# A different maker for the low parts of two groups of weights in an fp32 encoder

## The chip, the cores and the metric

The kernel runs on one core of a Trainium2 chip. A core has a matrix engine, TensorE (PE in the profile, its weight loads PEld), and VectorE (DVE), ScalarE (ACT), GpSimd (POOL) and SyncE (SP). Each works through its own list of instructions in order and waits on semaphores for the others. Matmul operands lie in SBUF and results in PSUM; DMA transfers are issued by SP and by POOL, each through its own queue. The metric is the device time of one execution in microseconds (us).

## The reference

Two layers of a transformer-like encoder on 512 tokens of width 1024, in fp32:

```python
for l in range(DEPTH):                                    # DEPTH = 2
    x = x + 0.5 * swiglu(rms_norm(x, ffn1_norm[l]), w_gate, w_up, w_down)
    h = rms_norm(x, mix_norm[l])
    p = h @ w_in[l]
    attn = mla_group(p[..., :o_kv], p[..., o_kv:o_pe], p[..., o_pe:o_cv], ...)
    conv = conv_group(p[..., o_cv:], ...)                 # GLU, causal convolution of 31 taps, LayerNorm, SiLU
    x = x + jnp.concatenate([attn, conv], axis=-1) @ w_out[l]
    x = x + 0.5 * swiglu(rms_norm(x, ffn2_norm[l]), w_gate, w_up, w_down)
    x = rms_norm(x, post_norm[l])
...
def swiglu(x, w_gate, w_up, w_down):
    return (jax.nn.silu(x @ w_gate) * (x @ w_up)) @ w_down  # hidden width 2816 = 22 x 128
```

## The kernel before

**Three matmuls for one.** Each fp32 operand is kept as two parts in a shorter format, `hi` (the value rounded by an ACT copy) and `lo` (what the rounding left). `mm3` does a product as hi·hi (L209), hi·lo of the activations (L210) and lo of the weights·hi (L211). So each weight tile, loaded from memory as plain fp32 into a buffer `raw` or `fr`, is split before use.

**Two ways to make a weight's low part.** The usual one: DVE subtracts `hi` from the loaded tile, in `load_w` at L164 and in `split_into` at L301. The other one: ACT writes the negative of the loaded tile's rounded value, and a DMA issued by POOL adds the same weights from memory on top of it. In `load_w` this is the kind `"sum"` (L160 and L161), in the FFN it is `subtracted` (L432 and L433), called by `summed`. In the first form of it the low part lies in the tile `weights`, a ring of four slots for `hi` and four for `lo`, whose writers are kept in their order by `in_turn`. In the second it lies in a buffer of the pool `ls`, of which there are two:

```python
lo = fpool.tile([P, WC], FR, tag="ls", name=nm("ls"), bufs=2)
```

**The FFN.** The 22 blocks of the hidden width are taken as 11 pairs, in chunks of 2, 3, 3, 2 and 1 pairs. `pair` makes one pair's activations by a scheme of seven products in place of eight, with quarters of the weights combined by DVE; two of its seven products (`b21`, `t4`) use `ls`. `down` multiplies a chunk's activations by the down weights in two halves `g`, also in seven products each: `b11` (quarter 0 of the weights), `b21` (quarter 1), `t2`, `t3`, `t1` (combinations), `t4` (quarter 3) and `b22`. Within `down`, `times` is one product; with a number `q` it takes `summed`, without one `split_into`. Before, `b21` and `t4` took `summed`, and the ACT copy and the DMA for `t4` were issued early, by `subtracted` ahead of `t3`. Quarters 0 and 1 are loaded by SP and later overwritten by the combinations.

**The two-pair stage.** The chunk of pairs 8 and 9 is the only one for which `np_`, the number of pairs in `down`, is 2; the others have `NP` = 3. Its weights are `wdr` (256 KB a quarter, 512 columns). It occurs in the first FFN of both layers and in the second FFN of the last one; the second FFN of the first layer joins the chunk with the next one and has no such stage. In the order of PE the pair after it (pair 10, `held`) stands ahead of the stage's `down`, and that pair's `t4` is the last reader of an `ls` buffer ahead of it. A tile scheduler sets the order of all instructions from the order in the code, its own estimates and the marks `issue_after`.

**The mixer's start.** `mix_body` begins with `groups` on the first two blocks `wcv` of the convolution's projection (512 KB each), and calls `norm` right after. While PE multiplies these, ACT squares the new `x` (L242) for the norm, POOL sums the squares (L246), and DVE makes the last low parts of the input (L223, in `split_scaled`) behind the residual sums of the FFN's end (L634).

Of the kernel before, what the change touches and what calls it, by code (L numbers as in the profile page):

```python
# [33 lines left out]
WC = 1024  # L34
# [6 lines left out]
NP = 3  # L41
# [42 lines left out]
def encoder_kernel(ctx: ExitStack, tc: tile.TileContext, xT, consts, vecs, rgain, wgu1, wd1, wdq1, wdr1,  # L84
# [11 lines left out]
    def nm(s):  # L96
        uid[0] += 1
        return f"{s}{uid[0]}"
# [7 lines left out]
    def bank():  # L106
        return psum.tile([P, S], FP, tag="ps", name=nm("ps"))
# [45 lines left out]
    def load_w(src, w, kind=""):  # L153
        raw = wpool.tile([P, WC], FP, tag="raw", name=nm("raw"), bufs=3)
        nc.sync.dma_start(out=raw[:, :w], in_=src)
        hi = part(0)
        order["cast"] = in_turn("h", lambda: A.copy(hi[:, :w], raw[:, :w]))  # L157
        lo = low()
        if kind == "sum":
            A.activation(lo[:, :w], raw[:, :w], AF.Copy, scale=-1.0)  # L160
            G.dma_start(out=lo[:, :w], in_=src, accum_op=ALU.add)  # L161
            return hi, lo
        e = G if kind in POOLW.split() else V
        in_turn(e, lambda: e.tensor_tensor(lo[:, :w], raw[:, :w], hi[:, :w].bitcast(FP), ALU.subtract))  # L164
        return hi, lo
# [4 lines left out]
    def part(j, moved=False):  # L170

        if was[j] and not moved:
            used[j] += 1
        was[j] = moved
        i = (j * WN + used[j] % WN) * WC + (WOFF[j] if moved else 0)
        used[j] += 1
        return weights[:, i:i + WC]
# [3 lines left out]
    def in_turn(key, make):  # L181

        with tc.issue_after(turns[key]) if key in turns else nullcontext():
            turns[key] = make().ins
        return turns[key]

    def low(moved=False):
        return part(1, moved)
# [19 lines left out]
    def mm3(o, lh, ll, rh, rl, first, last, free=False):  # L208
        T.matmul(o, lh, rh, start=first, stop=False, skip_group_check=free)  # L209
        T.matmul(o, lh, rl, start=False, stop=False, skip_group_check=free)  # L210
        order["mm"] = T.matmul(o, ll, rh, start=False, stop=last, skip_group_check=free).ins  # L211
        return order["mm"]
# [68 lines left out]
    def group(o, w, rhs, ks, n, ts=slice(0, S)):  # L281

        for k in ks:
            c = slice(k * P, (k + 1) * P)
            order["product"] = mm3(o, w[0][:, c], w[1][:, c], rhs[k][0][:, ts], rhs[k][1][:, ts], k == 0, k == n - 1)

    def groups(srcs, rhs, ws=None):

        ws = ws or [load_w(src, WC) for src in srcs]
        os = [bank() for _ in srcs]  # L290
        for ks in (range(KD - 1), range(KD - 1, KD)):
            for o, w in zip(os, ws):
                group(o, w, rhs, ks, KD)
        return os

    def split_into(q, src, w=WC):

        hi = part(0, True)
        in_turn("h", lambda: A.copy(hi[:, :w], src[:, :w]))  # L299
        lo = low(True)  # L300
        order["lo"] = in_turn(V, lambda: V.tensor_tensor(lo[:, :w], src[:, :w], hi[:, :w].bitcast(FP), ALU.subtract))  # L301
        return hi, lo
# [5 lines left out]
    def ffn_body(fpool, l, gx, norm, wgu, wd, wdq, wdr, gain, done, w0, halved, chunks):  # L308
# [20 lines left out]
        def quarters(w, n, first=False):  # L329

            a = quarter(), quarter() if first else late(), quarter(), quarter()
            for q in range(4):
                nc.sync.dma_start(out=a[q][:, :n], in_=w[q])
            return *a, late()
# [26 lines left out]
        def after(name):  # L361
            return tc.issue_after(order[name]) if name in order else nullcontext()
# [66 lines left out]
        def subtracted(w, src, n=WC):  # L429

            lo = fpool.tile([P, WC], FR, tag="ls", name=nm("ls"), bufs=2)
            A.activation(lo[:, :n], src[:, :n], AF.Copy, scale=-1.0)  # L432
            G.dma_start(out=lo[:, :n], in_=w, accum_op=ALU.add)  # L433
            return lo

        def summed(w, src, n=WC, lo=None):

            lo = subtracted(w, src, n) if lo is None else lo
            hi = part(0, True)
            in_turn("h", lambda: A.copy(hi[:, :n], src[:, :n]))  # L440
            return hi, lo
# [54 lines left out]
        def down(act, quarters_of):  # L496

            np_ = len(act)
            n = 2 * np_ * P
            for g in range(2):  # L500
                a11, a12, a21, a22, s3 = quarters(quarters_of(g), n)
                px, py, pz = bank(), bank(), bank()

                def times(o, src, name, start, q=None, lo=None):
                    hi, lo = split_into(name, src, n) if q is None else summed(quarters_of(g)[q], src, n, lo)
                    with tc.issue_after(order["pe"]):
                        for k in range(np_):
                            for i in range(2):
                                c = slice((i * np_ + k) * P, (i * np_ + k + 1) * P)
                                last = mm3(o[:, i * HS:(i + 1) * HS], hi[:, c], lo[:, c], *act[k][name],  # L510
                                           start and k == 0 and i == 0, k == np_ - 1, True)
                    order["pe"] = last

                def add(row, h, o, sign):
                    v = x[:, 4 * g + 2 * (1 - row):4 * g + 2 * (1 - row) + 2, h * HS:(h + 1) * HS]
                    return V.scalar_tensor_tensor(v, o.rearrange("p (m t) -> p m t", m=2), 0.5 * sign, v, ALU.mult,  # L516
                                                  ALU.add).ins
                times(px, a11, "b11", True)
                with after("u0"):
                    add(0, 0, px, 1)  # L520
                times(py, a12, "b21", True, 1)
                with after("u"):
                    add(0, 0, py, 1)
                with after("first") if g else nullcontext():
                    V.tensor_tensor(s3[:, :n], a11[:, :n], a21[:, :n], ALU.add)
                with after("first"):
                    V.tensor_tensor(a21[:, :n], a21[:, :n], a22[:, :n], ALU.add)
                    V.tensor_tensor(a11[:, :n], a11[:, :n], a21[:, :n], ALU.add)
                times(px, a11, "t2", False)
                order["second"] = add(1, 0, px, -1)  # L530
                with after("second" if g == 0 else "first"):
                    V.tensor_tensor(a12[:, :n], a12[:, :n], a11[:, :n], ALU.add)  # L532
                lo = subtracted(quarters_of(g)[3], a22, n)
                with after("u"):
                    times(pz, s3, "t3", True)
                add(1, 1, pz, 1)
                with after("v"), after("vh"):
                    times(px, a21, "t1", False)
                    order["first"] = add(1, 1, px, -1)
                    times(pz, a22, "t4", False, 3, lo)  # L540
                    add(1, 0, pz, 1)
                with after("v"), after("vh"):
                    times(px, a12, "b22", False)
                add(0, 1, px, 1)
# [13 lines left out]
        for p0, p1 in chunks:  # L558
# [46 lines left out]
            if p0 and not last:  # L605
                c = (p0 - CHUNKS[0][1]) // NP
                if p1 == chunks[-1][0] and p1 == CHUNKS[-1][0]:
                    held = pair(p1, False)
                down(act, (lambda g: wdq[l, g, c]) if c < NC else (lambda g: wdr[l, g]))
                continue  # L610
# [47 lines left out]
    def mix(l, gx, norm, done):  # L658
        with tc.tile_pool(name="k", bufs=4) as kpool:
            mix_body(kpool, l, gx, norm, done)  # L660

    def mix_body(kpool, l, gx, norm, done):
# [191 lines left out]
                                            ALU.mult).ins  # L854


        first = groups([wcv[l, 0], wcv[l, 1]], gx)
        rm = norm()
        for step in SEQ.split():
            if step == "R":  # L860
# [272 lines left out]
    gx = []  # L1133
# [21 lines left out]
    gx = [gx[KS.index(m)] for m in range(KD)]  # L1155
# [27 lines left out]
    for l in range(L):  # L1183
        nx, st1, done = follow(l, "gm")
        ffn(l, gx, norm, wgu1, wd1, wdq1, wdr1, vv(l, "g1"), done, w0 if l == 0 else None)
        gx = nx
        nx, st2, done = follow(l, "g2")
        mix(l, gx, Norm(st1), done)
        gx = nx
# [3 lines left out]
        if l + 1 < L:  # L1193
# [10 lines left out]
            gx = nx  # L1204
# [126 lines left out]
```

## Time and profile before

| | us |
|---|---|
| median of three runs (lowest, highest) | 1750.08 (1748.02, 1750.13) |
| the profiled execution | 1748.6 |
| its span, first to last instruction | 1746.8 |
| PE busy | 1729.1 |
| DVE busy | 1468.6 |
| ACT busy | 1097.4 |
| POOL busy | 394.2 |

The mean granted clock of TensorE was 0.998 of full speed. In the page's rows a time is the start of an instruction in us from the span's start, followed by its duration, engine, line of the program, operation, output <- inputs by the program's names, and shapes. A bracket at the end gives the idle time of that engine before the instruction and what ended it. Several like instructions that follow one another may share a row (x2). A row of a DMA issue gives the size and the median time from issue to landing.

### The profile page before, as it was taken

What the parts mean: (1) busy time and instruction counts of PE and PEld (TensorE: products, weight loads), DVE (VectorE), ACT (ScalarE), POOL (GpSimd) and SP (SyncE); (2) the same over time, 40 slices, a digit from 0 to 9 for tenths busy, and PEclk for the clock granted to TensorE, in tenths of its full rate; (3) what the DMA queues carried; (4) which work ended last, traced back from release to release, by engine and by line L of the source; (5) the groups of instructions that cost most, each with busy time, mean ns of one, the idle gap of its engine ahead of it and who ended that gap; (6) DMA issues with size and microseconds to landing.
All of it is one profiled execution on the core that took longest, in us unless ns stands there. A gap on an engine that the chain in (4) does not pass through costs nothing.

```text
span 1746.8 us, 31487 instructions
## 1 busy us (share of the span) xinstructions
PE 1729.1 (99%) x12486; PEld 1580.1 (90%) x12486; DVE 1468.6 (84%) x2099; ACT 1097.4 (63%) x1711; POOL 394.2 (23%) x327
## 2 busy tenths in 40 slices
PE   9999999999999999999999999999999999999998
PEld 8899999888678899999889999997976788999997
DVE  7888888888965989897679989888989568888887
ACT  5576756567953476756645757665778435767564
POOL 1001000348823001000310010013676410010002
PEclk9999999999999999999999999999999999999999
DMA  5567575424303467665426575754251125675753
GB/s 184 148 151 187 140 198 112 135 87 118 80 25 102 115 161 176 158 173 138 124 71 162 133 203 132 196 121 130 83 147 36 58 81 147 153 188 139 194 117 98
DMA packets 76852, 231.57 MB, mean 133 GB/s; under 512 B 8736, under 2 KB 12960, under 8 KB 76704
## 3 DMA queue, kind: packets, MB, share of 16 engines
q1 hardware_dynamic: 58704, 171.87, 30.8%
q0 software_dynamic: 17856, 57.68, 19.4%
q8 instruction: 98, 1.61, 0.4%
q14 instruction: 50, 0.41, 0.1%
q10 hardware_dynamic: 144, 0.00, 0.0%
HBM read 225.33 MB, written 2.10 MB: 130 GB/s over the span
## 4 chain that ended last, share of the span: by engine, by line
PE 69%; DVE 7%; ACT 2%; issue 2%; DMA 1%; DVEq 0%; ACTq 0%
PE ps L211 22%; PE ps L209 22%; PE ps L210 22%; DVE cv L999 1%; DVE mx L907 1%; PE ps L948 1%; PE ps L926 1%; DVE x L516 0%; DVE weights L164 0%; ACT weights L299 0%; PE ps L705 0%; DVE x L634 0%; DVE r L929 0%; DMA fr<-in_wgu 0%; ACT pr L1003 0%
## 5 line engine op out<-in xcount | busy, mean ns | idle before, releaser
L210 PE MATMUL ps<-r,weights 128*128 128x256 f32 (+1 forms) x2620 | 810.6, 309 | 2.6 <-DVE r L223 2.6
L209 PE MATMUL ps<-r,weights 128*128 128x256 f32 (+1 forms) x2620 | 807.5, 311 | 0.2
L211 PE MATMUL ps<-r,weights 128*128 128x256 f32 (+1 forms) x2380 | 741.2, 313 | 6.0 <-DVE weights L301 3.7
L210 PEld LDWEIGHTS ps<-r,weights 128*128 128x128 f32 x2620 | 492.1, 188 | 35.5 <-DVE r L223 4.4
L209 PEld LDWEIGHTS ps<-r,weights 128*128 128x128 f32 x2620 | 492.2, 188 | 33.4 <-issue 2.0
L211 PEld LDWEIGHTS ps<-r,weights 128*128 128x128 f32 x2380 | 446.8, 188 | 38.6 <-DVE weights L301 5.0
L209 PE MATMUL ps<-xj,weights 128*128 128x256 f32 x864 | 238.5, 276 | 0.0
L210 PE MATMUL ps<-xj,weights 128*128 128x256 f32 x864 | 238.5, 276 | 0.0
L299 ACT CAST weights<-fr 128x1024 fp32r<-128x1024 f32 (+2 forms) x178 | 168.5, 946 | 96.7 <-DVE fr L453 43.0
L157 ACT CAST weights<-raw 128x1024 fp32r<-128x1024 f32 (+4 forms) x124 | 112.1, 916 | 176.1 <-PE ps L210 112.3
L301 DVE TENSOR_TENSOR weights<-fr,weights 128x1024 fp32r<-128x1024 f32 (+2 forms) x178 | 195.4, 1098 | 31.5 <-ACT weights L299 31.5
L433 POOL DMA_DIRECT2D ls<-in_wgu x72 | 62.5, 868 | 703.7 <-ACT ls L432 633.3
L164 DVE TENSOR_TENSOR weights<-raw,weights 128x1024 fp32r<-128x1024 f32 (+4 forms) x108 | 120.8, 1126 | 65.1 <-ACT weights L157 64.3
L210 PEld LDWEIGHTS ps<-xj,weights 128*128 128x128 f32 x864 | 162.2, 188 | 0.0
L209 PEld LDWEIGHTS ps<-xj,weights 128*128 128x128 f32 x864 | 162.2, 188 | 0.0
L211 PE MATMUL ps<-xj,ls 128*128 128x256 f32 x576 | 159.0, 276 | 0.0
L301 DVE TENSOR_TENSOR weights<-raw,weights 128x1024 fp32r<-128x1024 f32 (+2 forms) x112 | 122.1, 1091 | 14.1 <-ACT weights L299 13.9
L299 ACT CAST weights<-raw 128x1024 fp32r<-128x1024 f32 (+2 forms) x112 | 105.2, 939 | 42.8 <-DVE raw L532 23.5
L1005 POOL TENSOR_TENSOR y<-y,pr 128x495 f32<-128x495 f32 (+29 forms) x90 | 119.3, 1329 | 45.8 <-ACT pr L1003 40.5
L432 ACT ACTIVATE ls<-fr 128x1024 fp32r<-128x1024 f32 (+2 forms) x62 | 59.9, 967 | 98.7 <-PE ps L211 63.0
L516 DVE SCALAR_TENSOR_TENSOR x<-ps,x 128x512 f32<-128x512 f32 x154 | 105.8, 687 | 8.7 <-PE ps L211 7.8
L211 PEld LDWEIGHTS ps<-xj,ls 128*128 128x128 f32 x576 | 108.1, 188 | 0.0
(260 smaller groups left out, 3021.0 us busy)
## 6 DMA issues: line engine op xcount, KB each, us to landing
fr<-in_wgu SPq DMA_DIRECT2D x112, 512.0 KB, 4.7
ls<-in_wgu POOLq DMA_DIRECT2D x72, 512.0 KB, 7.1
raw<-in_wgu SPq DMA_DIRECT2D x62, 512.0 KB, 5.3
fr<-in_wdq SPq DMA_DIRECT2D x48, 384.0 KB, 4.5
ls<-in_wdq POOLq DMA_DIRECT2D x32, 384.0 KB, 6.3
raw<-in_wd SPq DMA_DIRECT2D x32, 256.0 KB, 2.8
raw<-in_wcv SPq DMA_DIRECT2D x16, 512.0 KB, 3.8
raw<-in_wout SPq DMA_DIRECT2D x16, 512.0 KB, 3.3
```

The costliest lines, as they stand in the source:

```text
L157: order["cast"] = in_turn("h", lambda: A.copy(hi[:, :w], raw[:, :w]))
L164: in_turn(e, lambda: e.tensor_tensor(lo[:, :w], raw[:, :w], hi[:, :w].bitcast(FP), ALU.subtract))
L209: T.matmul(o, lh, rh, start=first, stop=False, skip_group_check=free)
L210: T.matmul(o, lh, rl, start=False, stop=False, skip_group_check=free)
L211: order["mm"] = T.matmul(o, ll, rh, start=False, stop=last, skip_group_check=free).ins
L299: in_turn("h", lambda: A.copy(hi[:, :w], src[:, :w]))
L301: order["lo"] = in_turn(V, lambda: V.tensor_tensor(lo[:, :w], src[:, :w], hi[:, :w].bitcast(FP), ALU.subtract))
L432: A.activation(lo[:, :n], src[:, :n], AF.Copy, scale=-1.0)
L433: G.dma_start(out=lo[:, :n], in_=w, accum_op=ALU.add)
L516: return V.scalar_tensor_tensor(v, o.rearrange("p (m t) -> p m t", m=2), 0.5 * sign, v, ALU.mult, ALU.add).ins
L907: V.tensor_reduce(mx[:, i:i + 1], o, axis=AX.X, op=ALU.max, negate=True)
L1005: order["conv"] = G.tensor_tensor(ys[c][:, s:], ys[c][:, s:], pr[:, s:], ALU.add).ins
```

## The change

The first product of each half of the two-pair stage, `b11`, gets its weights' low part by `summed` in place of `split_into`; stages with three pairs stay as they are. And the first two blocks of the convolution's projection are loaded with the kind `"sum"` in each layer.

```diff
@@ down
-                times(px, a11, "b11", True)
+                times(px, a11, "b11", True, 0 if np_ < NP else None)
@@ mix_body
-        first = groups([wcv[l, 0], wcv[l, 1]], gx)
+        first = groups([wcv[l, 0], wcv[l, 1]], gx, [load_w(wcv[l, i], WC, "sum") for i in range(2)])
```

Over the program DVE has 10 instructions less, ACT 10 more and POOL 8 more rows of DMA issues and sums (the two DMAs of a layer's mixer share a row). The order of SP is the same.

On ACT, in the two-pair stage of the first layer's first FFN, one piece of the difference (`fr_3522` is quarter 0 of the first half, `raw_3523` quarter 1, `fr_3525` quarter 3):

```order
 L457 ACTIVATE t_3367<-t_3332 128x256
 L216 CAST r_3290<-t_3281 128x512
-L299 CAST weights<-fr_3522 128x512
+L440 CAST weights<-fr_3522 128x512
 L426 COPY t_3424<-ps_3305 128x512
 L440 CAST weights<-raw_3523 128x512
 L426 COPY e_3396<-ps_3303 128x512
-L432 ACTIVATE ls_3585<-fr_3525 128x512
+L432 ACTIVATE ls_3551<-raw_3523 128x512
 L299 CAST weights<-fr_3522 128x512
 L471 ACTIVATE t_3483<-e_3396 128x512
```

The L432 that stands here made the operand of `t4` before, and makes that of `b21` now; the one ahead of this piece made `b21`'s before and makes `b11`'s now.

On ACT at the start of the first layer's mixer (`raw_` of L157 is a `wcv` block). Before:

```order
L196 CAST weights_106<-raw395_3776 128x1024
L157 CAST weights_106<-raw447_3931 128x1024
L157 CAST weights_106<-raw448_3935 128x1024
L222 ACTIVATE r397_3788<-x_74,vec_76 128x512
L239 ACTIVATE r399_3792<-x_74 128x512
L157 CAST weights_106<-raw455_3999 128x1024
```

After:

```order
L196 CAST weights_106<-raw397_3780 128x1024
L157 CAST weights_106<-raw449_3935 128x1024
L160 ACTIVATE weights_106<-raw449_3935 128x1024
L157 CAST weights_106<-raw450_3940 128x1024
L160 ACTIVATE weights_106<-raw450_3940 128x1024
L222 ACTIVATE r399_3792<-x_74,vec_76 128x512
```

Two L160 have come in, each behind the cast of its block; on DVE the two L164 of these blocks are gone, and on POOL the two DMAs stand ahead of the first L246.

On DVE, where the second layer's first FFN begins its first pair by `pair` (L452 to L454 combine quarters of the weights, L634 is a residual sum and L1225 multiplies a block of `x` by the rate of the layer's last norm; their `ps` are products of the down weights). Before:

```order
L452 TENSOR_TENSOR fr1345_10114<-fr1345_10114,fr1346_10115 128x1024
L301 TENSOR_TENSOR weights_106<-fr1343_10112,weights_106 128x1024
L634 SCALAR_TENSOR_TENSOR x_74<-ps1322_9993,x_74 128x512
L1225 TENSOR_TENSOR x_74<-x_74,r1264_9720 128x512
L453 TENSOR_TENSOR fr1343_10112<-fr1343_10112,fr1345_10114 128x1024
L634 SCALAR_TENSOR_TENSOR x_74<-ps1327_10018,x_74 128x512
L1225 TENSOR_TENSOR x_74<-x_74,r1264_9720 128x512
L454 TENSOR_TENSOR fr1344_10113<-fr1344_10113,fr1343_10112 128x1024
L301 TENSOR_TENSOR weights_106<-fr1343_10112,weights_106 128x1024
```

After:

```order
L452 TENSOR_TENSOR fr1347_10120<-fr1347_10120,fr1348_10121 128x1024
L634 SCALAR_TENSOR_TENSOR x_74<-ps1324_9999,x_74 128x512
L1225 TENSOR_TENSOR x_74<-x_74,r1266_9726 128x512
L634 SCALAR_TENSOR_TENSOR x_74<-ps1329_10024,x_74 128x512
L1225 TENSOR_TENSOR x_74<-x_74,r1266_9726 128x512
L301 TENSOR_TENSOR weights_106<-fr1345_10118,weights_106 128x1024
L634 SCALAR_TENSOR_TENSOR x_74<-ps1333_10048,x_74 128x512
L1225 TENSOR_TENSOR x_74<-x_74,r1266_9726 128x512
L453 TENSOR_TENSOR fr1345_10118<-fr1345_10118,fr1347_10120 128x1024
L634 SCALAR_TENSOR_TENSOR x_74<-ps1338_10073,x_74 128x512
L1225 TENSOR_TENSOR x_74<-x_74,r1266_9726 128x512
L454 TENSOR_TENSOR fr1346_10119<-fr1346_10119,fr1345_10118 128x1024
```

The first L301, the low part of the pair's first product, has moved behind two more pairs of L634 and L1225.

## The prediction

> **What bounds the kernel now.** I read the page's head first, then the chain that ended last, then the waits of PE.
>
> ```profile
> span 1746.8 us, 31487 instructions
> PE 1729.1 (99%) x12486; PEld 1580.1 (90%) x12486; DVE 1468.6 (84%) x2099; ACT 1097.4 (63%) x1711; POOL 394.2 (23%) x327
> ...
> PE 69%; DVE 7%; ACT 2%; issue 2%; DMA 1%; DVEq 0%; ACTq 0%
> ```
>
> TensorE (PE) is busy for 1729.1 of 1746.8 us, so the change, which leaves the number of matmuls as it is, can win at most 17.7 us, and only where PE now waits for something that the change makes earlier. VectorE time as such is worth nothing: taken off DVE, it counts only at the places where PE waits for DVE. The waits of PE name two of those that lie at the edited places:
>
> ```profile
> PE ps L211 <- DVE weights L301: 3.7, 4, 1.2
> PE ps L210 <- DVE r L223: 2.6, 2, 1.4
> ```
>
> The columns are total, number of waits and longest. Three of the four waits on L301 come once in each two-pair stage; the two on L223 come once per layer at the mixer's start. These are what can be won. What can be lost stands in the rows of the same stages, below.
>
> **The two-pair stages: what the edit removes and adds.** There are three such stages (first FFN of both layers, second FFN of the last), each with two halves, so six quarters change. Per quarter DVE loses one L301 on 512 columns, and ACT gains one L432, POOL one DMA issue of L433; the ACT cast only changes its line. The buffer is what matters: `ls` has two buffers, before the change a half took two of them (`b21`, `t4`), and now it takes three (`b11`, `b21`, `t4`). So each L432 must wait until the product two places earlier has read its buffer. Here is the first stage before:
>
> ```profile
> 301.46 0.28 PE L211 MATMUL ps<-xj,ls 128*128 128x256 f32 x1
> 301.77 0.64 ACT L432 ACTIVATE ls<-fr 128x512 fp32r<-128x512 f32 x1 [2.13 <-PE ps L211]
> 302.70 0.86 POOL L433 DMA_DIRECT2D ls<-in_wdr  x1 [9.13 <-ACT ls L432]
> ...
> 305.88 0.28 PE L211 MATMUL ps<-r,ls 128*128 128x256 f32 x1
> ...
> 312.45 0.28 PE L211 MATMUL ps<-r,ls 128*128 128x256 f32 x1
> 312.76 0.64 ACT L432 ACTIVATE ls<-fr 128x512 fp32r<-128x512 f32 x1 [0.81 <-PE ps L211]
> 313.69 0.86 POOL L433 DMA_DIRECT2D ls<-in_wdr  x1 [4.22 <-ACT ls L432]
> ...
> 315.51 0.28 PE L211 MATMUL ps<-r,ls 128*128 128x256 f32 x1
> ...
> 316.79 0.28 PE L210 MATMUL ps<-r,weights 128*128 128x256 f32 x1
> 318.26 0.39 PE L211 MATMUL ps<-r,weights 128*128 128x256 f32 x1 [1.19 <-DVE weights L301]
> ```
>
> The chain is plain in rows 301.46 to 302.70: the last matmul of the held pair's `t4` ends at 301.74, ACT writes the freed buffer from 301.77, the DMA is issued at 302.70. Before, this chain made the first half's `t4` operand, due late. Now the first half's `b11` takes the buffer that was free early, and this chain makes `b21`, whose first matmul that reads `ls` is row 305.88. In the second half the same happens again: the chain that follows the first half's `t4` (rows 312.45 to 313.69) made the second half's `t4` operand before; now it makes the second half's `b21`, whose first reader is row 315.51. So the transfer has 305.88 − 302.70 = 3.18 us in the first half and 315.51 − 313.69 = 1.82 us in the second. How long it takes is shown for the very issues that stood in these places, in order the first stage's two, then those at 1167.3, 1178.2, 1699.9 and 1710.9 in the other two stages:
>
> ```profile
> ls<-in_wdr POOLq DMA_DIRECT2D x1, 256.0 KB, 4.1
> ...
> ls<-in_wdr POOLq DMA_DIRECT2D x1, 256.0 KB, 4.4
> ...
> ls<-in_wdr POOLq DMA_DIRECT2D x1, 256.0 KB, 4.1
> ...
> ls<-in_wdr POOLq DMA_DIRECT2D x1, 256.0 KB, 4.7
> ...
> ls<-in_wdr POOLq DMA_DIRECT2D x1, 256.0 KB, 3.9
> ...
> ls<-in_wdr POOLq DMA_DIRECT2D x1, 256.0 KB, 5.4
> ```
>
> PE waits for the landing plus about 0.1 us (an estimate: the cast at 325.46 below starts so long after its load, issued at 321.03, has landed in 4.3). In the first half that is 4.1 − 3.18 + 0.1 = 1.0, 1.0 and 0.8 us in the three stages. In the second half the chain starts from a matmul that this first stall has itself put off, so issue and need move together, and the stall is 4.4 − 1.82 + 0.1 = 2.7, then 3.0 and 3.7 us. I take the other two stages to have the first one's distances, since they are the same program. Together 12.2 us. Against it stands what is won: the stall at 318.26, 318.26 − 316.79 − 0.11 (the step of one matmul, as from 312.45 to the next) = 1.36 us, goes in all three stages, 4.1 us, because PE arrives there 3.7 us later while its operand's maker, DVE, waits for nothing that is late. Net **+8.1 us**.
>
> Bounds: with the shortest landing of these (3.9) in every place the stalls are 0.8 + 2.2 a stage, net +4.9 us in all. The longest landing of this DMA in before is the one at 292.71:
>
> ```profile
> ls<-in_wdr POOLq DMA_DIRECT2D x1, 256.0 KB, 6.8
> ```
>
> That one runs beside four plain loads; in every place it would give 3.7 + 5.1 a stage, net +22. No load is issued near 302.70 or 313.69, so I stay by the like rows and leave that end to a rival. The two other new operands (first half's `t4`, second half's `b11`) come 0.5 to 0.8 us before their need by the same reckoning; late landings there would also add. ACT's extra 0.64 us a quarter costs nothing: ACT is busy 63%, and it waited 2.13 us before the row at 301.77. What stands behind a waiting L432 on ACT is hidden too; the nearest is `t2`'s cast in the second half, now behind the L432 for `t4`, which waits for `b11` to end at about 315.5 + 1.0: three instructions of some 0.65 us (L432, the cast, L301) make its operands ready by 318.5, and `t2` starts at 316.64 + 3.7 = 320.3.
>
> [...]
>
> **The mixer's start.** In each layer the first two convolution blocks lose an L164 on DVE (1.2 us each or more) and gain an L160 on ACT and an L161 on POOL.
>
> ```profile
> 324.66 0.34 SPq L155 DMA_DIRECT2D raw<-in_wcv  x1
> 325.46 1.05 ACT L157 CAST weights<-raw 128x1024 fp32r<-128x1024 f32 x1 [0.68 <-DMA raw<-in_wcv]
> 328.47 1.05 ACT L157 CAST weights<-raw 128x1024 fp32r<-128x1024 f32 x1 [1.95 <-DMA raw<-in_wcv]
> ...
> 335.86 0.61 PE L209 MATMUL ps<-r,weights 128*128 128x512 f32 x2
> ...
> 343.38 0.39 PE L209 MATMUL ps<-r,weights 128*128 128x512 f32 x1
> 344.98 0.50 PE L210 MATMUL ps<-r,weights 128*128 128x512 f32 x1 [1.22 <-DVE r L223]
> ...
> 1209.32 0.50 PE L210 MATMUL ps<-r,weights 128*128 128x512 f32 x1 [1.37 <-DVE r L223]
> ```
>
> Won: PE's stall at 344.98 (344.98 − 343.38 − 0.23 = 1.37 us) and the one at 1209.32 (its 1.37 us of idle and 0.16 of the matmuls' overlap, 1.5 us) go, since DVE has two long instructions less ahead of L223 and PE comes later: −2.9 us. Lost: the second block's low part. Its raw load (324.66) waits for a buffer whose last reader comes behind the two-pair stage, so it moves by that stage's +2.4: issued 327.1, landed 3.8 later, cast from 331.0 (328.47 + 2.4, rounded up), then L160 to about 333.0, and the DMA 0.3 later, as from 301.77 + 0.64 to 302.70. The nearest rows for a 512 KB accumulating transfer into `weights` are those of `wout`; the first line is the median of all eight, the second the one issued at 429.3, the third the middle of that one and its neighbour issued 0.6 later, so that the neighbour took 2 x 7.6 − 5.6 = 9.6:
>
> ```profile
> L160 ACT ACTIVATE weights<-raw 128x1024 fp32r<-128x1024 f32 x8 | 8.4, 1053 | 0.0
> ...
> weights<-in_wout POOLq DMA_DIRECT2D x8, 512.0 KB, 7.8
> ...
> weights<-in_wout POOLq DMA_DIRECT2D x1, 512.0 KB, 5.6
> ...
> weights<-in_wout POOLq DMA_DIRECT2D x2, 512.0 KB, 7.6
> ```
>
> 333.3 + 7.8 + 0.1 = 341.2. PE needs it at the tenth matmul of the two blocks: they start with the second matmul of row 335.86, at 336.1, now 338.5, and nine steps of 0.23 make 340.5. So 0.7 us a layer is lost (0 with 5.6, 2.5 with 9.6), and the stage nets −2.9 + 1.4 = **−1.5 us** (−2.9 to +2.1). POOL has no other work there until its sums (L246), which wait for ACT's L242 in any case.
>
> **The second layer's first FFN pair.** No line of it changes, but the scheduler puts DVE's L301 of its first product behind two updates of `x` (L634 and L1225, twice); the next L301 slides with it.
>
> ```profile
> 938.29 1.22 DVE L301 TENSOR_TENSOR weights<-fr,weights 128x1024 fp32r<-128x1024 f32 x1
> 939.42 0.69 DVE L634 SCALAR_TENSOR_TENSOR x<-ps,x 128x512 f32<-128x512 f32 x1
> ...
> 940.12 0.51 PE L211 MATMUL ps<-r,weights 128*128 128x512 f32 x2
> ...
> 944.09 1.22 DVE L301 TENSOR_TENSOR weights<-fr,weights 128x1024 fp32r<-128x1024 f32 x1
> ...
> 945.81 0.28 PE L211 MATMUL ps<-r,weights 128*128 128x256 f32 x1
> ```
>
> Before, the first ended at 939.5; its reader is the second matmul of row 940.12, at 940.35. Each L634 or L1225 takes DVE 0.60 from start to start (939.42 to the next at 940.02), so the L301 starts at 938.29 + 2.4 = 940.7 and ends at 941.9: PE stalls 1.6. The second L301 starts 2.4 later too, 946.5, and ends at 947.7; its reader, 945.81 + 1.6 = 947.4, stalls 0.3. **+1.9 us**; 0 if PE reaches that matmul later than in this trace, 2.9 if the updates moved ahead find their products late.
>
> **The sum.** 8.1 − 1.5 + 1.9 = +8.5 us. Against the profiled execution's own 1748.6 us (its span and 1.8 around it) that is 1757.1; the median of the runs shown, 1750.08, lies 1.5 above it, which makes 1758.6. I say 1758.0.
>
> **The rivals** (times against the runs' median).
> *It gets faster.* The accumulating transfers land in time and only DVE's relief is left: −4.1 − 2.9 + 1.9 = −5.1 us, 1745. What speaks for it is that the waits on DVE are real; against it that the second half's transfer has 1.82 us, and the shortest of the six rows took 3.9. It decides in the second half: faster needs both halves' stalls of a stage below 1.36 us, so a landing within about 3.1 us there. And it needs 1.7 us for all of it. 4%.
> *Nothing measurable.* An accumulating transfer takes as long as a plain load of the same size:
>
> ```profile
> fr<-in_wdr SPq DMA_DIRECT2D x18, 256.0 KB, 2.9
> raw<-in_wcv SPq DMA_DIRECT2D x16, 512.0 KB, 3.8
> ```
>
> With 2.9 the first halves don't stall, the second halves stall 1.2 and win 1.36 (−0.5 for three), the mixer's block is in time (−2.9), and the pair costs 1.9: −1.5 us, 1748.6. For it: the bytes are the same. Against it: all six like rows of POOL are longer, by 1.0 to 2.5. The same result comes from the rows' favourable ends together (+4.9 − 2.9 + 0 = +2.0, 1752). 10%. [...]
> *Much slower.* More DMAs share the queue, and landings lengthen to 5.5 us at each place of the stages: 2.4 + 3.8 − 1.36 a stage is +14.5, with the mixer's +2.1 and +1.9 about +18.5, 1768.6. For it: 5.4 in the third stage. Against it: only 10 DMAs are added to 327 POOL instructions, and issues 4 us or more apart. 12%.
>
> **How the numbers follow.** The forecast has 74%, and its own range is the terms' nearer ends, +4 to +13 (1753.5 to 1763). To hold 8 in 10 with part of the neighbours I give 1752.0 to 1764.0. A measurement of this kernel tells about 0.2%, 3.5 us, from no change. Faster by more: 4%; within: 10%; slower: the forecast and the much slower case, 86%.
>
> **What would show it.** In the new profile PE's L211 on `ls` waits for the DMA `ls<-in_wdr` twice a stage, about 1 us, then about 3; the waits on L301 in those stages are gone and the one on L223 too; L211 waits for `weights<-in_wcv` under 1 us at the mixer's start; and one wait of 1.6 us on L301 stands in the second layer's first pair. If the `in_wdr` transfers land within 3.1 us, or PE reaches `b21` later than I think, the forecast is wrong.

## The result and the profile after

The changed kernel takes 1760.23 us (median of four runs, 1759.05 to 1762.41) against 1749.24 us of the kernel before (four runs): a ratio of 1.0059 with a 95% interval of 1.0047 to 1.0071, 11 us slower. A later set of runs gave 1761.59 against 1749.47, ratio 1.0066 (1.0052 to 1.0080).

First the head of the page of the kernel after, and its waits of PE (total, number, longest):

```profile
span 1760.6 us, 31510 instructions
PE 1733.8 (98%) x12486; PEld 1583.7 (90%) x12486; DVE 1463.8 (83%) x2089; ACT 1104.0 (63%) x1721; POOL 401.2 (23%) x337
...
PE ps L211 <- DMA ls<-in_wdr: 9.3, 6, 2.8
PE ps L211 <- DVE weights L301: 3.1, 7, 1.5
PE ps L211 <- DMA weights<-in_wcv: 2.3, 2, 1.2
```

DVE is busy 4.8 us less, as meant, and PE waits for other things. The wait on L223 is gone from the list. Six waits on the stage's accumulating transfers are new, two in each two-pair stage, and two on those of the mixer. Of the waits on L301 the longest has grown to 1.5 us; it stands in the second layer's first pair, and none is left in the stages.

The first stage in the timeline of the kernel after, with the rows that answer to those shown of before:

```profile
303.91 0.86 POOL L433 DMA_DIRECT2D ls<-in_wdr  x1 [9.12 <-ACT ls L432]
...
308.08 0.39 PE L211 MATMUL ps<-r,ls 128*128 128x256 f32 x1 [0.83 <-DMA ls<-in_wdr]
...
314.69 0.28 PE L211 MATMUL ps<-r,ls 128*128 128x256 f32 x1
...
315.00 0.64 ACT L432 ACTIVATE ls<-raw 128x512 fp32r<-128x512 f32 x1 [0.81 <-PE ps L211]
...
315.93 0.86 POOL L433 DMA_DIRECT2D ls<-in_wdr  x1 [4.11 <-ACT ls L432]
...
319.98 0.39 PE L211 MATMUL ps<-r,ls 128*128 128x256 f32 x1 [2.06 <-DMA ls<-in_wdr]
...
320.89 0.42 PE L209 MATMUL ps<-r,weights 128*128 128x256 f32 x1
321.11 0.42 PE L210 MATMUL ps<-r,weights 128*128 128x256 f32 x1
```

The chain is the one of the prediction: PE frees the buffer (314.69), ACT writes it (315.00), POOL issues (315.93), and PE waits for the landing (319.98). The last two rows hold what the prediction did not have. The matmuls there take 0.42 us and not 0.28, and follow each other in 0.22 us and not in 0.11. The granted clock in a view by stretches says why (the columns that matter: us, PE busy with its instructions, and behind the engines' columns the granted clock, as a share of full speed, then the DMA share and GB/s):

```profile
320.80:324.30 3.50, 3.50 (x19) 3.50 (x18) 1.29 (x2) 0.80 (x2) 0.00 (x0) 0.51 0.81 206
1191.50:1194.60 3.10, 3.10 (x15) 3.10 (x16) 0.64 (x2) 0.62 (x1) 0.00 (x0) 0.50 0.90 199
1728.80:1732.00 3.20, 3.20 (x31) 3.20 (x30) 2.47 (x4) 1.25 (x2) 0.00 (x0) 1.00 0.87 212
```

After the long wait PE ran at half clock for 3.41 us in the first two stages, and at full clock in the third. In the kernel before the only such stretches lie in the program's last 10 us, from 1737.45 and from 1744.28, behind the third stage; the program's end has them in every profile here (in this one from 1751.06 and from 1757.88).

Both programs issue 12486 matmuls in nearly the same order, so the start of the n-th one can be compared in the two traces. Where the distance grows is where the time was lost:

| place | forecast, us | this profile, us |
|---|---|---|
| first stage | +2.4 | +3.5 |
| second stage | +2.6 | +3.9 |
| third stage | +3.1 | +2.0 |
| mixer starts, both | −1.5 | −0.7 |
| second layer's first pair | +1.9 | +2.4 |
| sum | +8.5 | +11.0 |
| everywhere else | 0 | +2.8 |

The last line belongs to places that the change does not edit: 0.65 us of it lies at the program's start, and most of the rest in steps of some 0.45 us at single matmuls of other stages, where PE waits for an L301. At the one followed back, a plain load of `in_wdq` landed some 0.5 us later. In a second profile of the changed kernel the same line is −0.5 us up to the end of the third stage; another +1.0 stands behind it, at the program's end, where the half clock lasted 6.83 us in one stretch. The mixer's starts win nothing in that profile (0.0 us in all).

### The profile page after: what moved, and what is told of

Read it like the earlier page. It is cut to its first block, busy times and chain, and to the rows that moved or that the text cites. A ratio compares the mean times of both kernels' runs of the same rounds, so it can differ in the third digit from the quotient of the medians.

```text
span 1760.6 us, 31510 instructions
## 1 busy us (share of the span) xinstructions
PE 1733.8 (98%) x12486; PEld 1583.7 (90%) x12486; DVE 1463.8 (83%) x2089; ACT 1104.0 (63%) x1721; POOL 401.2 (23%) x337
## 5 line engine op out<-in xcount | busy, mean ns | idle before, releaser
L299 ACT CAST weights<-fr 128x1024 fp32r<-128x1024 f32 (+2 forms) x172 | 164.6, 957 | 90.8 <-DVE fr L453 41.4
L157 ACT CAST weights<-raw 128x1024 fp32r<-128x1024 f32 (+4 forms) x124 | 112.1, 917 | 171.6 <-PE ps L210 112.3
L301 DVE TENSOR_TENSOR weights<-fr,weights 128x1024 fp32r<-128x1024 f32 (+2 forms) x172 | 191.0, 1110 | 32.2 <-ACT weights L299 32.2
L164 DVE TENSOR_TENSOR weights<-raw,weights 128x1024 fp32r<-128x1024 f32 (+4 forms) x104 | 113.3, 1099 | 61.9 <-ACT weights L157 61.1
L301 DVE TENSOR_TENSOR weights<-raw,weights 128x1024 fp32r<-128x1024 f32 (+2 forms) x112 | 121.9, 1089 | 13.6 <-ACT weights L299 13.4
L432 ACT ACTIVATE ls<-fr 128x1024 fp32r<-128x1024 f32 (+2 forms) x68 | 63.6, 936 | 99.9 <-PE ps L211 60.7
```

## The experiments

**One part alone.** First the stages without the mixer, then the mixer without the stages.

```diff
# only_stage: the first part of the change and not the second
-                times(px, a11, "b11", True)
+                times(px, a11, "b11", True, 0 if np_ < NP else None)
```

> The two-pair stages alone take the new low parts; the mixer is as before. My theory (the third operand of a half finds no free buffer of the pool with two, and its accumulating DMA lands after PE needs it): two waits of PE on the in_wdr transfers per stage, 1.0 and 2.2 to 2.9 us, then up to 1.6 us at half clock in some stages, the second layer's first pair 2.4 us later: +11 to +13 us against the kernel before, that is about all of the change's loss or slightly more. Rival A (the loss is the mixer's two accumulating DMAs): within 3 us of before.

Measured: 1759.65 us against 1749.80, ratio 1.0054 (1.0042 to 1.0067), +9.9 us. The waits of PE in its profile:

```profile
PE ps L211 <- DMA ls<-in_wdr: 9.4, 6, 2.4
PE ps L210 <- DVE r L223: 2.6, 2, 1.3
...
PE ps L211 <- DVE weights L301: 1.6, 1, 1.6
```

The six waits on `in_wdr` and the long one in the first pair belong to this part; the mixer waits on L223 as before. The loss is the stage part's, a little under what was expected of it, since in this profile no stage has the half clock.

```diff
# only_mixer: the second part of the change and not the first
-        first = groups([wcv[l, 0], wcv[l, 1]], gx)
+        first = groups([wcv[l, 0], wcv[l, 1]], gx, [load_w(wcv[l, i], WC, "sum") for i in range(2)])
```

> The two convolution blocks alone are loaded with the kind sum; the stages are as before. My theory: PE loses its wait on L223 (1.4 and 1.5 us) and gets one of 1 to 2 us on the second block's accumulating DMA in each layer: -1 to +2 us. Rival A: +8 us or more. Rival B (what slows the stages is that POOL's queue and ACT are loaded more in all places): a few us slower.

Measured: 1748.22 us, ratio 0.9991 (0.9982 to 1.0000). PE's wait on L223 is gone, and

```profile
PE ps L211 <- DMA weights<-in_wcv: 3.0, 2, 1.7
```

has taken its place, at about the same size. So the mixer's part alone is a swap of one wait for another; rival A is out. The median is 1.6 us lower, a little more than the 1 us expected; in the profile, whose span is 1.1 us shorter, PE is level with before until the program's last 12 us, so the mixer did not win it there.

**The buffer or the work?** Two kernels keep every added ACT copy and DMA but give the stage's operands another place.

```diff
# shared_buffer, against the changed kernel: b11 and b21 as two halves of one buffer
-        def subtracted(w, src, n=WC):
+        def subtracted(w, src, n=WC, lo=None):
-            lo = fpool.tile([P, WC], FR, tag="ls", name=nm("ls"), bufs=2)
+            lo = fpool.tile([P, WC], FR, tag="ls", name=nm("ls"), bufs=2) if lo is None else lo
...
-                times(px, a11, "b11", True, 0 if np_ < NP else None)
+                both = [None, None]
+                if np_ < NP:
+                    t = fpool.tile([P, WC], FR, tag="ls", name=nm("ls"), bufs=2)
+                    both = [subtracted(quarters_of(g)[i], (a11, a12)[i], n, t[:, i * n:(i + 1) * n]) for i in range(2)]
+                times(px, a11, "b11", True, 0 if np_ < NP else None, both[0])
...
-                times(py, a12, "b21", True, 1)
+                times(py, a12, "b21", True, 1, both[1])
```

> As the changed kernel, but in the two-pair stage the low parts of b11 and b21 are the two halves of one buffer of the pool, so that a half takes two buffers as before the change and none waits for the product just ahead of it. The same ACT copies and the same DMAs are issued. My theory: PE's waits on in_wdr go (0 to 0.6 us each in the second halves), the half clock goes, and the wait on L301 in the stages is gone too; what is left is the second layer's first pair (+2.4) and the mixer: -3 to +2 us against before, 9 to 13 faster than the changed kernel. Rival B (the added transfers and copies are slow wherever they stand): the waits stay at 3 us a stage, +8 us or more.

```diff
# in_ring, against the changed kernel, in times()
-                    hi, lo = split_into(name, src, n) if q is None else summed(quarters_of(g)[q], src, n, lo)
+                    if q == 0:
+                        hi = part(0, True)
+                        in_turn("h", lambda: A.copy(hi[:, :n], src[:, :n]))
+                        lo = low(True)
+                        A.activation(lo[:, :n], src[:, :n], AF.Copy, scale=-1.0)
+                        G.dma_start(out=lo[:, :n], in_=quarters_of(g)[q], accum_op=ALU.add)
+                    else:
+                        hi, lo = split_into(name, src, n) if q is None else summed(quarters_of(g)[q], src, n, lo)
```

> As the changed kernel, but the low part of b11 in the two-pair stage is written (by the same ACT copy and the same kind of DMA) into the four-slot ring of weights in place of the pool of two. Here the scheduler also leaves the second layer's first pair as before. My theory: no wait on in_wdr above 0.5 us, no half clock, no wait on L301 in the stages, none of the 1.6 us in the first pair: -5 to -1 us against before. Rival B: +5 us or more.

`shared_buffer` took 1748.20 us, ratio 0.9991 (0.9982 to 1.0000), 12 us less than the changed kernel with the same copies and transfers (1.6 us under the kernel before of its own set of runs, where the changed kernel was 11 us above); `in_ring` took 1750.88, ratio 1.0005 (0.9996 to 1.0014). The waits of PE of the one, then of the other:

```profile
PE ps L211 <- DMA weights<-in_wcv: 3.5, 2, 2.1
PE ps L211 <- DVE weights L301: 1.9, 4, 0.7
```

```profile
PE ps L211 <- DMA weights<-in_wcv: 3.1, 2, 1.5
...
PE ps L211 <- DVE weights L301: 1.2, 3, 0.4
PE ps L211 <- DMA weights<-in_wdr: 1.1, 2, 0.8
```

No wait on `ls<-in_wdr` is left in either, and no half clock ahead of the program's end. So it is neither the added work nor the DMA's length as such, but where the operand finds a free buffer: rival B is out. What remained of my expectation failed at one point: `in_ring` should have won 1 to 5 us and won nothing that can be measured. Its trace says where that went. The wait on L301 in the stage did not vanish but fell:

```profile
317.88 0.39 PE L211 MATMUL ps<-r,weights 128*128 128x256 f32 x1 [0.40 <-DVE weights L301]
```

This is the row of `shared_buffer` that stands for 318.26 before; start to start it is 0.56 us late there and 1.36 before; in `in_ring` it is 0.55 to 0.56 us late in all three stages. One DVE instruction less in the second half is worth 0.8 us, not 1.36. And in the ring the second half's `b11` comes 0.45, 0.2 and 0.95 us late in the three stages, more than the 0.5 us allowed for. The mixer gives nothing, as above.

**The two halves apart.**

```diff
# first_halves; second_halves has g == 1
-                times(px, a11, "b11", True)
+                times(px, a11, "b11", True, 0 if np_ < NP and g == 0 else None)
```

> Of the change only b11 of the first half of each two-pair stage; mixer as before. My theory: in each stage one wait of 1.0 us on in_wdr for b21 of the first half, none in the second half, where the buffers come round as before; the wait on L301 in the second half stays, at 0.4 to 1.36 us; the second layer's first pair, where the scheduler puts one pair of updates ahead of L301 and not two, costs 0.4 to 1 us: +1 to +4 us against before. Rival (each of the two halves costs alike, whatever buffer it finds): +5 to +6, with waits of 2 us in the stage.

> Of the change only b11 of the second half of each two-pair stage; mixer as before. My theory: no wait on in_wdr in the first half; one of 2.2 to 2.7 us in the second, where b21 waits for the buffer of the first half's t4; the wait on L301 (1.36) goes: +1 us and a little more a stage, with the second layer's first pair +4 to +6 us against before, more by 1.5 us for each stage after which the matmuls run at half clock. Rival (each half costs alike): +5 to +6 with 2 us.

`first_halves`: 1752.66 us against 1749.59, ratio 1.0013 (1.0004 to 1.0022). `second_halves`: 1757.28, ratio 1.0043 (1.0030 to 1.0057). The waits of the one and of the other:

```profile
PE ps L211 <- DVE weights L301: 3.5, 3, 1.2
PE ps L211 <- DMA ls<-in_wdr: 2.8, 3, 0.9
```

```profile
PE ps L211 <- DMA ls<-in_wdr: 8.1, 3, 3.0
```

As told by the chain: one wait of about 1 us a stage in the first case, one of 2.6 to 3.2 us in the second, where it also takes the place of the wait on L301. A delay in the first half does not shorten the wait on L301: it stays at its full 1.2 us. DVE's work there hangs on PE and moves with it: in the first stage DVE itself waits 0.71 us for PE at 308.83, just behind the late `b21`. `second_halves` costs 7.7 us, above what I expected; one of its stages has the half clock.

**The half clock.** The wait of the second half was lengthened by a second transfer.

```diff
# landing_twice, against second_halves; "again" is set for b21 of the second half (the lines that pass it on are left out)
             G.dma_start(out=lo[:, :n], in_=w, accum_op=ALU.add)
+            if again:
+                G.dma_start(out=lo[:, :n], in_=w, accum_op=ALU.add)
             return lo
```

> As second_halves, but the accumulating transfer of b21's low part in the second half is issued a second time behind the first (this low part then is wrong by one times the weights). It lengthens the one wait in question by one transfer, 4 to 4.5 us, and is a test of the half clock: if a wait of PE of some 2 to 3 us is what sets it off, and only where it falls well, waits of 6 to 7 us set it off in all three stages. My theory: +12 to +13.5 us against second_halves by the transfers, and 1.5 us more for each of three stages at half clock, +16 to +18 in all. Without the half clock +12 to +13.5.

Measured: 1776.79 us, 19.5 us above `second_halves`. PE's waits are 24.2 us in three; start to start they are 8.5, 7.9 and 8.3 us where `second_halves` has 3.2, 2.8 and 2.6, so the second transfer cost 16.1 us, 5.4 each and not 4 to 4.5. The 3.4 us left are about the size of two more stages at half clock; together they put the time above the 16 to 18 us expected. Behind each wait the clock was half (in the trace it falls before the wait is over, in the first stage at 318.04 where PE goes on at 324.08):

```profile
324.50:328.00 3.50, 3.50 (x18) 3.50 (x18) 0.69 (x1) 0.62 (x1) 0.00 (x0) 0.50 0.05 8
1198.90:1201.80 2.90, 2.90 (x15) 2.90 (x15) 0.69 (x1) 0.62 (x1) 0.00 (x0) 0.50 0.06 11
1739.90:1744.70 4.80, 4.80 (x24) 4.80 (x24) 0.84 (x2) 0.98 (x2) 0.00 (x0) 0.50 0.02 5
```

The changed kernel was then profiled once more:

> The changed kernel itself, once more. Waits on in_wdr and in_wcv as in its first profile (9.3 and 2.3 us); +9 to +13 us. If the half clock of the first profile (two stages) depends on where the wait falls, this profile has it in other stages or in none, and its span differs from the first by about 1.5 us for each.

```profile
319.80:322.30 2.50, 2.50 (x13) 2.50 (x13) 0.35 (x1) 0.51 (x1) 0.00 (x0) 0.50 0.83 177
1190.30:1192.70 2.40, 2.40 (x13) 2.40 (x13) 0.33 (x1) 0.49 (x1) 0.00 (x0) 0.50 0.99 257
1725.90:1728.60 2.70, 2.70 (x14) 2.70 (x14) 0.54 (x1) 0.62 (x1) 0.00 (x0) 0.50 0.80 168
```

This time all three stages have it, after waits of 2.6, 2.9 and 2.4 us start to start, and the third costs 3.5 us instead of 2.0. PE's waits on `in_wdr` and `in_wcv` are 10.0 and 2.5 us. The span, 1760.7 us, is nevertheless no longer than the first profile's 1760.6, against the 1.5 us expected for one stage more: the places outside the stages and the mixer, told above, make up for it. The same three places of `only_stage`, after waits of 2.3, 2.6 and 2.4 us:

```profile
319.30:322.80 3.50, 3.50 (x32) 3.50 (x33) 2.13 (x4) 1.24 (x2) 0.00 (x0) 1.00 0.87 197
1189.30:1192.80 3.50, 3.50 (x31) 3.50 (x32) 2.10 (x4) 1.24 (x2) 0.00 (x0) 1.00 0.81 204
1724.70:1728.20 3.50, 3.50 (x31) 3.50 (x32) 2.07 (x4) 1.24 (x2) 0.00 (x0) 1.00 0.88 174
```

So the half clock came with waits of 2 to 3 us in some executions and not in others, with waits of 8 us in all three, and ahead of the program's end with none of up to 1.9 us. The traces show what goes with it. In each of the twelve, all changes of the clock lie whole multiples of 3.413 us apart: in the first profile after, the two stretches start at 320.87 and 1191.27 us, 255 such steps from one to the other; in the kernel before the changes behind the third stage lie at 1737.45, 1740.86 and 1744.28. If the whole execution is divided by this grid, the clock of a window goes with how long PE was busy in the window just before it. Three pairs of neighbouring windows, of the first profile after, of `ring_one_block` and of `second_halves`:

```profile
317.46:320.87 3.41, 1.35 (x12) 1.15 (x11) 2.69 (x5) 2.18 (x4) 0.86 (x1) 1.00 0.78 94
320.87:324.28 3.41, 3.41 (x18) 3.41 (x17) 1.29 (x2) 0.78 (x2) 0.00 (x0) 0.50 0.80 208
...
343.44:346.85 3.41, 1.46 (x7) 0.91 (x6) 3.41 (x4) 0.00 (x0) 1.87 (x1) 1.00 0.44 145
346.85:350.26 3.41, 3.41 (x10) 2.63 (x9) 0.93 (x2) 0.00 (x0) 0.00 (x0) 0.50 0.02 8
...
317.57:320.98 3.41, 1.73 (x14) 1.73 (x15) 1.23 (x3) 0.98 (x3) 0.28 (x1) 1.00 0.71 129
320.98:324.39 3.41, 3.41 (x32) 3.41 (x31) 3.04 (x5) 0.94 (x2) 0.00 (x0) 1.00 0.35 123
```

The last pair belongs to the longest of these short waits, 3.2 us, from 316.1 to 319.25. The grid cuts it in two: PE is busy for 1.73 us in the window that holds its end and for 2.11 us in the one that holds its start, and the clock stays full. In all twelve traces, ahead of the program's last 18 us, ten windows at full clock had PE busy for at most 1.46 us, and half clock followed each of them; it followed none of the some 6,000 others, the least busy of which has 1.62 us. In these traces the half clock goes with how much of the wait lies in one window, and the windows lie differently in different executions: with steps of 870.40 / 255 = 3.4133 us, their edges are 0.02 us behind a whole number of steps from the span's start in the first profile after, and 2.10 us behind in `ring_one_block`. This is read from traces, not from an experiment that moved the window, so that the one decides the other is my estimate. It does not carry over to the program's last 18 us, where the matmuls are of other shapes and half clock came also after windows with PE busy for 2.4 to 2.8 us. Nor need PE stand still for the whole window: in `ring_one_block` it was busy for 43% of it (1.46 of 3.41 us), and half clock followed.

**Can the gain be had?**

```diff
# ring_one_block, against in_ring
-        first = groups([wcv[l, 0], wcv[l, 1]], gx, [load_w(wcv[l, i], WC, "sum") for i in range(2)])
+        first = groups([wcv[l, 0], wcv[l, 1]], gx, [load_w(wcv[l, i], WC, "" if i else "sum") for i in range(2)])
```

> As in_ring, but only the first of the two convolution blocks is loaded with the kind sum; the second block's low part is DVE's again. PE no longer waits for in_wcv (1.7 us in each layer there); DVE has one instruction of 1.2 us less ahead of L223 than before, so the wait on L223 (1.4 and 1.5 us before) is between 0 and 0.5 us. 1.5 to 3 us faster than in_ring, 2 to 5 us faster than before. If PE's wait on in_wcv only hid a wait on L223 of the same size, nothing is won against in_ring.

```diff
# shared_second, against shared_buffer
-                if np_ < NP:
+                if np_ < NP and g:
...
-                times(px, a11, "b11", True, 0 if np_ < NP else None, both[0])
+                times(px, a11, "b11", True, 0 if np_ < NP and g else None, both[0])
```

> As shared_buffer, but in the second half of each stage alone; the first half's b11 is DVE's again, as before the change; both mixer blocks with the kind sum. My theory: no wait on in_wdr, the wait on L301 in the stage at 0.56 us as in shared_buffer (0.8 less than before), 0.5 us in the second layer's first pair, the mixer as in only_mixer: -2 to 0 us against before. If the first halves' new work had cost anything in shared_buffer, this one is faster than that by as much.

`ring_one_block`: 1749.48 us against 1749.59, ratio 1.0001 (0.9992 to 1.0010). `shared_second`: 1749.74 against 1749.47, ratio 1.0001 (0.9992 to 1.0010). In the first of them the wait on DMA is gone from the mixer and the wait on L223 is back, 2.0 and 1.3 us:

```profile
PE ps L210 <- DVE r L223: 3.3, 2, 2.0
```

The alternative named in its expectation holds: one L164 less is not enough to free DVE there. Neither kernel beats the one before by anything that these runs can tell; the fastest of all, `shared_buffer` and `only_mixer`, have intervals that reach up to 1.0000.

## Why the prediction was right, and where its steps were not

The forecast, slower by the late operands of the two-pair stages, is what happened, and 1760.23 lies in the range. That the total came as close as +11 us against +8 is in part luck: the waits were 1.9 us shorter than forecast, while the half clock, which the sum did not have, added about 3 and the mixer won 0.8 less. Step by step:

- **The buffer chain** was right. The experiments show it as the cause: with the same work and a free buffer the 11 us are gone. The waits are those of the working, start to start 1.0, 0.8 and 1.2 us in the first halves (1.0, 1.0, 0.8 forecast) and 2.2, 2.9 and 2.1 in the second (2.7, 3.0, 3.7), 10.3 us in all and not 12.2. What differs is landings: 4.0, 4.7 and 3.9 us in the second halves, where I had taken 4.4, 4.7 and 5.4. The 5.4 of the third stage was one execution's, not the place's.
- **The sum left out the half clock.** Net of the stall won, the stages cost 9.4 us in the first profile, of which about 3 are the half clock (some 16 and 14 matmuls at 0.1 us more). Ahead of the program's last 10 us no row of before shows one; no wait there was so long. In the first two stages this turned an over-estimate into an under-estimate. The forecast's third stage, which did not have it in this profile, was 1.1 too high.
- **"Goes in all three stages, 4.1 us"** is right in the changed kernel, but only since PE is late there. DVE's relief alone takes 0.8 of the 1.36 us. So the rival "it gets faster" counted on too much: where no operand was late (`shared_buffer`, `shared_second`), the stages won 0.9 us each and no more.
- **The mixer.** The wait on L223 went, as forecast. The second block came 1.4 and 1.3 us late and not 0.7, since its transfer took 8.6 and 8.8 us where I had the median of 7.8:

```profile
weights<-in_wcv POOLq DMA_DIRECT2D x1, 512.0 KB, 8.6
```

- **The second layer's first pair**: 1.6 us forecast and 1.64 measured for the first L301. Here are the rows of the kernel after:

```profile
943.55 0.69 DVE L634 SCALAR_TENSOR_TENSOR x<-ps,x 128x512 f32<-128x512 f32 x1
944.16 0.68 DVE L1225 TENSOR_TENSOR x<-x,r 128x512 f32<-128x512 f32 x1
944.76 1.22 DVE L301 TENSOR_TENSOR weights<-fr,weights 128x1024 fp32r<-128x1024 f32 x1
...
946.03 0.39 PE L211 MATMUL ps<-r,weights 128*128 128x256 f32 x1 [1.47 <-DVE weights L301]
...
951.88 0.39 PE L209 MATMUL ps<-r,weights 128*128 128x256 f32 x1 [0.31 <-ACT t L426]
```

  The second stall is there too, 0.5 us, but it is ACT's copy L426 that PE waits for and not the next L301. In the kernels whose scheduler kept the order of before (`only_mixer`, `in_ring`, `ring_one_block`) no wait stands at this place. With one pair of updates ahead of the L301 (`first_halves`, `second_halves`, `shared_second`) the first wait is at most 0.3 us and the 0.5 us stays, and with two (the changed kernel's second profile, `only_stage`, `shared_buffer`) the first wait is 1.3, 1.7 and 0.8 us. The order alone was not changed by itself in any run, so this is how order and wait go together, not a proof.
- **The landings.** The six rows of the profile that the sum went by decided rightly: the transfers of 256 KB of this kind took 3.9 to 6.8 us in the kernel before and 3.8 to 6.4 us in the kernel after, and none took less than 3.7 us in any run here.

## What to carry to other kernels

Moving work off a busy engine is priced by the waits of the bound engine, and by what the new way needs to start: count the buffers per stage, and follow each new operand back to the product that must end before its buffer is free. Where a change makes an engine wait that never waited long, allow for what the wait itself brings; here waits of TensorE of 2.2 and 2.9 us came with 3.41 us at half clock each, which cost some 1.6 and 1.4 us more; in the 3.41 us just ahead of the half clock TensorE had been busy for 1.35 and 0.79 us. And before a transfer is used to relieve an engine, look at how long that very transfer has taken in the same stage; two operands in one buffer cost no SBUF and took the whole loss away.

## What the runs showed of the hardware

- Granted clock 0.50 for 3.41 us after TensorE had waited 2.2 to 2.9 us, in six of twelve second halves (two of three in the first profile after, three in the second, none in `only_stage`, one in `second_halves`) whose waits were 2.1 to 3.2 us, once after a wait of 2.1 us on L223 (`ring_one_block`), and, for 6.8 to 10.2 us, with all three waits of 8 us. The changes of clock lie on a grid of 3.413 us; ahead of the program's last 18 us half clock followed exactly on the windows in which PE was busy for at most 1.46 us, ten of some 6,000 in twelve traces.
- Plain loads took longer beside accumulating transfers, 5.9 and 8.2 us against 4.3 and 4.4 in the first layer. Two loads of the mixer's next blocks, each issued by SP 0.3 us ahead of an accumulating transfer of 512 KB, are the first two rows (after); the same loads before are the last two. In all profiles with two such transfers in a mixer start these loads took 5.0 to 9.6 us, in those without 3.4 to 4.6:

```profile
raw<-in_wcv SPq DMA_DIRECT2D x1, 512.0 KB, 5.9
...
raw<-in_wcv SPq DMA_DIRECT2D x1, 512.0 KB, 8.2
```

```profile
raw<-in_wcv SPq DMA_DIRECT2D x1, 512.0 KB, 4.3
...
raw<-in_wcv SPq DMA_DIRECT2D x1, 512.0 KB, 4.4
```
